# The first keys' sums stay in PSUM banks, B's projection moves behind the first stage, and a fourth shift block is summed along rows

## The chip, the cores and the metric

The kernel runs on one core of a Trainium2 chip. The metric is the device time of the whole program in microseconds. The engines are TensorE (PE, with its weight loads PEld), VectorE (DVE), ScalarE (ACT), GpSimd (POOL) and SyncE (SP), which here only issues DMAs; PSUM has 8 banks of 128 x 512 fp32.

## The reference

Two layers over 256 latent tokens and 256 context tokens of width 2048, all in fp32. The part of the first layer that the change is in:

```python
shift, scale, gate = adaln(c, ada_w[i], ada_b[i])            # silu(c) @ w + b, three parts
h = modulate(rms_norm(x, norm_g[i]), shift[:, None], scale[:, None])
shift_c, scale_c, gate_c = adaln(c_ctx, ada_w[i], ada_b[i])
hc = modulate(rms_norm(ctx, norm_g[i]), shift_c, scale_c)
p = h @ w_in                                                 # 2048 x 14400: Q, gate, z, K, V, x, B, C, dt
pc = hc @ w_in[:, base:]                                     # the context needs K, V, x, B, C, dt only
q = rms_norm(heads(cols(p, COL_Q, ...)), q_norm_g)           # 16 heads of 128
k = rms_norm(heads(cols(p, COL_K, ...)), k_norm_g)
```

Then come neighbourhood attention with the context's keys, a bidirectional SSD scan in 8 groups (its B and C go through a convolution of 5 taps), gating and the output projection. The second layer is a gated short convolution. Only the first layer's start is touched.

## The kernel before

Every fp32 operand is split into a high part (fp32r) and the rest, and a product takes three matmuls: high x high, low x high, high x low. A weight of 512 KB (two row blocks of 128 x 512) is loaded into a raw buffer; ScalarE casts its high part into a place (`split`, line 422) and VectorE subtracts to get the low part (`low_part`, line 429). There are three places (w_95, w_96, w_97 in the listings below). The raw buffers are five, raw_90 to raw_94, and in the first stage four spare ones (two halves of PT, xtm, yi). SP issues all loads in one order; a load waits there until its buffer is free, and the loads behind it wait too.

A planner writes the program: Python tasks ask for an engine and for operands, a model of times (`Plan`) tells when they will be ready, and each instruction is put at the end of its engine's list when the model holds it to be due. What is put there is fixed; each engine runs its list in order.

The first stage starts before the modulated input h is known, and builds it block by block. There are eight blocks of 256 input channels; I count blocks from 1 and the stage's steps j from 0, so block 3 belongs to step 2. For a block, its scale and shift (256 values each, for latent and context) are needed. TensorE makes one of them as a product with the padded conditioning vectors: four loads of 512 KB from ada0, 32 narrow matmuls (`cpad`, line 742), a copy, two transposes and a sum (`ada_gen`). For the blocks in `DOTS` the shift is made by VectorE instead (`dot_gen`): the weights lie transposed, the conditioning vectors are broadcast to all partitions (the two loads `full`, line 850), and eight multiply-and-sum instructions along rows (line 859) and a reduction give the shift. `dot_gen` begins when step 2 begins. Then h of the block is written as hH and hL (lines 780 to 792), and step j adds the block's share to

- K and V of the first four heads, for four tiles of 128 rows (two latent, two context): each tile is six matmuls into a bank, and `part_gen` adds the bank to a running sum in SBUF: ScalarE copies at step 0, VectorE adds later (line 818). K's sums lie in the tiles sz and gt, V's in Vt.
- Q for the two latent tiles, kept in two banks (psQ) over all steps,
- B of the first SSD group (`b_part`), kept in two banks (psB0): twelve matmuls.

So four banks remain for K, V and modulation. A row tile of h needs the token rows transposed first (x, lines 640 to 650); the context's last tile comes late in step 0. After step 7 the stage is over, and the program goes on with the first gate (128 x 256 tiles), the dt columns, C, x and z of the first SSD group, attention heads and so on, each projection with the weights of the whole 2048 rows in a row.

## Time and profile before

| | us |
|---|---|
| runs: median, lowest, highest of 3 | 1741.1, 1739.43, 1741.53 |
| profiled execution: span from first to last instruction | 1738.3 |
| TensorE busy | 1717.7 (99%) |
| VectorE busy | 1253.3 (72%) |
| ScalarE busy | 776.2 (45%) |
| mean granted TensorE clock | 1.000 |

The profiled execution's own time is its span; the median of the runs lies 2.8 us above it. Busy is the time in which at least one instruction of the engine was under way. Matmuls overlap, so two that start 0.23 us apart each show some 0.39 us. In the views of the order of time a line has its start and length, the engine, the line of the kernel, the operation, out<-in, the shape and the count, and in brackets the idle time before it and what ended it. A window's line has, after its length, the busy time and count of PE, PEld, DVE, ACT and POOL, then the granted clock, the busy share of the DMA engines and GB/s.

### The profile page before, as it was taken

How to read it: one execution, taken by the hardware profiler on the slowest of the kernel's cores; microseconds unless marked ns; L12 is line 12 of the kernel's file. 1: busy time of each engine (PE TensorE's matmuls, PEld its weight loads, DVE VectorE, ACT ScalarE, POOL GpSimd, SP SyncE). 2: the span in 40 equal slices, each digit the busy share in tenths (PEclk: the TensorE clock that was granted, in tenths of full speed). 3: DMA queues.
4: the chain of work that ended last, by engine and by line, in shares of the span. 5: the costliest groups of instructions: out<-in, count | busy, mean ns of one | idle time of the engine just before them, and what ended most of it. 6: DMA issues, size and time to landing. Idle time of an engine off the chain costs nothing.

```text
span 1738.3 us, 24820 instructions
## 1 busy us (share of the span) xinstructions
PE 1717.7 (99%) x9255; PEld 1451.5 (84%) x9255; DVE 1253.3 (72%) x2108; ACT 776.2 (45%) x1367; POOL 33.2 (2%) x28
## 2 busy tenths in 40 slices
PE   6999999999999999999999999999999999999999
PEld 4777989889888889888888898888888888888887
DVE  5698787877576877676877687887668667665654
ACT  6434544445243445243435243665445344444442
POOL 0000100001000001000000000000000000000000
PEclk9999999999999999999999999999999999999999
DMA  9987644566754765755766567767867888776763
GB/s 375 366 319 271 206 135 142 180 209 187 228 183 151 234 210 183 227 188 164 230 221 195 191 196 248 258 225 254 280 204 260 267 272 284 246 241 191 248 213 114
DMA packets 192391, 391.03 MB, mean 225 GB/s; under 512 B 16200, under 2 KB 45960, under 8 KB 192016
## 3 DMA queue, kind: packets, MB, share of 16 engines
q1 hardware_dynamic: 184960, 382.88, 67.8%
q10 hardware_dynamic: 7312, 6.59, 1.2%
q8 instruction: 72, 1.18, 0.3%
q14 instruction: 47, 0.39, 0.1%
HBM read 379.79 MB, written 9.62 MB: 224 GB/s over the span
## 4 chain that ended last, share of the span: by engine, by line
PE 96%; DMA 2%; DVE 2%; issue 0%; SPq 0%; ACT 0%; POOL 0%; DVEq 0%; ACTq 0%
PE bank L196 93%; PE bank L200 3%; DMA raw<-in_ada 1%; DMA full<-dram_crow 1%; DVE csb L859 0%; DVE w L429 0%; DVE raw L859 0%; SPq L603 0%; DVE gt L818 0%; DVE yi L859 0%; DVE tmp L623 0%; DVE hL L792 0%; DVE sz L818 0%; DVE tmp L2116 0%; SPq L383 0%
## 5 line engine op out<-in xcount | busy, mean ns | idle before, releaser
L422 ACT CAST w<-raw 128x1024 fp32r<-128x1024 f32 (+1 forms) x344 | 359.8, 1047 | 554.7 <-PE bank L196 462.0
L429 DVE TENSOR_TENSOR w<-raw,w 128x1024 fp32r<-128x1024 f32 (+1 forms) x344 | 417.2, 1216 | 239.5 <-ACT w L422 238.2
L196 PE MATMUL bank<-hH,w 128*128 128x256 f32 (+1 forms) x2064 | 487.0, 325 | 0.0
L196 PE MATMUL bank<-w,hH 128*128 128x512 f32 x1280 | 405.7, 396 | 4.0 <-ACT hH L780 2.5
L196 PEld LDWEIGHTS bank<-hH,w 128*128 128x128 f32 x2064 | 345.3, 188 | 32.1 <-issue 1.7
L196 PE MATMUL bank<-hL,w 128*128 128x256 f32 (+1 forms) x1040 | 335.0, 322 | 0.0
L196 PEld LDWEIGHTS bank<-w,hH 128*128 128x128 f32 x1280 | 237.1, 188 | 56.3 <-DVE gt L818 3.4
L196 PE MATMUL bank<-w,hL 128*128 128x512 f32 x640 | 250.0, 391 | 0.2
L196 PEld LDWEIGHTS bank<-hL,w 128*128 128x128 f32 x1040 | 196.5, 189 | 14.5
L196 PE MATMUL bank<-w,h 128*128 128x512 f32 x768 | 178.2, 390 | 0.0
L196 PEld LDWEIGHTS bank<-w,h 128*128 128x128 f32 x768 | 144.1, 188 | 29.7
L888 DVE CUSTOM_DVE_ANT_0 raw<-raw,csb 128x1024 f32<-128x1024 f32 x128 | 155.3, 1218 | 11.9 <-DMA raw<-in_adaT 9.1
L196 PEld LDWEIGHTS bank<-w,hL 128*128 128x128 f32 x640 | 120.2, 188 | 25.7 <-DVE hL L792 0.9
L196 PE MATMUL bank<-w,mix 128*128 128x512 f32 x588 | 137.8, 391 | 0.0
L196 PEld LDWEIGHTS bank<-w,mix 128*128 128x128 f32 x588 | 109.7, 188 | 22.2 <-issue 0.3
L1371 DVE SCALAR_TENSOR_TENSOR tmp<-bank,cwh,tmp 128x508 f32<-128x508 f32 (+1 forms) x96 | 71.3, 746 | 1.9
L196 PE MATMUL bank<-KL,h 128*128 128x512 f32 x264 | 63.9, 390 | 0.0
L196 PEld LDWEIGHTS bank<-KL,h 128*128 128x128 f32 x264 | 49.5, 188 | 10.2
L196 PE MATMUL bank<-wH,h 128*128 128x512 f32 x168 | 55.7, 391 | 0.0
L196 PE MATMUL bank<-QT,h 128*128 128x512 f32 x168 | 55.7, 391 | 0.0
L429 DVE TENSOR_TENSOR wL<-raw,wH 128x1024 fp32r<-128x1024 f32 x31 | 37.9, 1223 | 23.9 <-ACT wH L422 23.8
L429 DVE TENSOR_TENSOR QL<-raw,QT 128x1024 fp32r<-128x1024 f32 x32 | 39.1, 1223 | 22.1 <-ACT QT L422 21.8
(306 smaller groups left out, 1962.3 us busy)
## 6 DMA issues: line engine op xcount, KB each, us to landing
raw<-in_w_in SPq DMA_DIRECT2D x196, 512.0 KB, 3.8
raw<-in_adaT SPq DMA_DIRECT2D x128, 512.0 KB, 4.8
raw<-in_sc_in SPq DMA_DIRECT2D x128, 512.0 KB, 4.7
raw<-in_w_out SPq DMA_DIRECT2D x64, 512.0 KB, 4.5
raw<-in_ada SPq DMA_DIRECT2D x35, 512.0 KB, 7.7
raw<-in_sc_out SPq DMA_DIRECT2D x32, 512.0 KB, 4.7
raw<-in_w SPq DMA_DIRECT2D x16, 512.0 KB, 5.5
tmp<-dram_csr SPq DMA_DIRECT2D x32, 256.0 KB, 5.2
```

Of the source, the lines that this page charges most:

```text
L196: E(T.matmul(o, l, r, start=start, stop=stop, skip_group_check=True))
L200: E(T.transpose(o, i, ident if k == 128 else ident[:k, :k]))
L422: E(S.copy(H, v))
L429: E(V.tensor_tensor(out=Lo, in0=v, in1=H.bitcast(F32), op=ALU.subtract))
L888: E(V.tensor_tensor_reduce(out=raw, in0=raw, in1=csb, scale=1.0, scalar=0.0, op0=ALU.mult, op1=ALU.add, accum_out=gp[:, h, m:m + 1]))
L1371: E(V.scalar_tensor_tensor(out=do, in0=di, scalar=cwh[:, 32 * k + ch:32 * k + ch + 1], in1=do, op0=ALU.mult, op1=ALU.add))
```

## The change

K's four sums stay in four banks (psK) from step 0 to step 7, as Q's do, and the norm of the keys reads the banks; V is summed as before. That frees sz and gt, which serve as a fourth weight place (wH_101, wL_104) until 24 weights are used, the end of the first stage. K and V tiles alternate in a step. B of the first SSD group is no longer part of the stage: it is projected after the dt columns like the later groups' B, from four loads of 512 KB in place of eight of 256 KB. `DOTS` is 2, 4, 6, 7 in place of 4, 5, 7 (blocks 3, 5, 7, 8 in place of 5, 6, 8), with the weights of these blocks laid out accordingly.

```diff
--- before.py
+++ after.py
@@ -172,10 +172,12 @@
 
 
     xrow = [st([128, D], "KT", name="x0")]
-    QT, Vt, gt = st([128, 4, 256], "QT", F32R), st([128, 4, 512], "Vt"), st([128, 4, 256], "gt")
+    QT, Vt = st([128, 4, 256], "QT", F32R), st([128, 4, 512], "Vt")
+    WH.append(st([128, 1024], "gt", F32R, name="wH3"))
     xrow.append(st([128, D], "KL", name="x1"))
     QL = st([128, 4, 256], "QL", F32R)
-    sz, xtm, yi = st([128, 4, 256], "sz"), st([128, 2, 512], "xtm"), st([128, 4, 256], "yi")
+    WL.append(st([128, 1024], "sz", F32R, name="wL3"))
+    xtm, yi = st([128, 2, 512], "xtm"), st([128, 4, 256], "yi")
     PTs = st([128, 2, 4, 256], "PT")
     PT = [PTs[:, k] for k in range(2)]
 
@@ -360,7 +362,7 @@
     onload = {}
 
     later = deque()
-    DOTS = (4, 5, 7)
+    DOTS = (2, 4, 6, 7)
     started = [False]
     ngem = [0]
 
@@ -394,11 +396,17 @@
 
     lows = deque()
 
-    free_w, in_use = deque(range(NW)), deque()
+    free_w, in_use = deque(range(NW + 1)), deque()
+    NFIRSTW = 24
+
+    def free_place():
+        return next((w for w in free_w if w != NW or pos["split"] < NFIRSTW), None)
 
     def place():
-        in_use.append(free_w.popleft())
-        return in_use[-1]
+        w = free_place()
+        free_w.remove(w)
+        in_use.append(w)
+        return w
 
     def split():
         k = pos["split"]
@@ -457,7 +465,7 @@
         if hold[0]:
             return
         lows_try()
-        while free_w and pos["split"] in RAW:
+        while free_place() is not None and pos["split"] in RAW:
             if plan.ready([RAW[pos["split"]][1]]) > max(plan.t["PE"], plan.t["ACT"]) + 300:
                 return
             split()
@@ -481,6 +489,8 @@
         w = in_use.popleft()
         if w is not None:
             free_w.append(w)
+        if pos["use"] == NFIRSTW:
+            free_w.remove(NW)
         splits_try()
 
 
@@ -537,7 +547,6 @@
     loads.append(lambda: x_load(3))
     loads.append(lambda: E(DMA.dma_start(sm[:, NFIRST:], small[:, NFIRST:])))
     loads.append(lambda: E(DMA.dma_start(cs_[:, CFIRST:], const[:, CFIRST:])))
-    weight(w_in, 0, 2, COL_B, 256)
     q_ada(1)
     dots = deque()
 
@@ -559,7 +568,6 @@
             q_ada(j + 1, *((0,) if j + 1 in DOTS else (0, 1)))
         dot_load()
         w_seg(j, CQ)
-        weight(w_in, j * 256, 2, COL_B, 256)
     loads.append(later_loads)
 
     order = list(range(0, 6)) + list(range(8, 16)) + [6, 7]
@@ -568,7 +576,7 @@
     q_proj(w_in, CG(0), 512)
     for r0 in (0, 1024):
         weight(w_in, r0, 8, COL_DT, 64)
-    for j_ in ssd_cols(0)[1:]:
+    for j_ in ssd_cols(0):
         q_proj(*j_)
     for a in range(1, 4):
         qk = [(w_in, CQ(a), 512), (w_in, CK(a), 512)]
@@ -805,8 +813,6 @@
     statk, statq = st([128, 16], "statk"), st([128, 8], "statq")
 
 
-    szf, gtf = sz.rearrange("p a b -> p (a b)"), gt.rearrange("p a b -> p (a b)")
-    parK = [szf[:, 0:512], szf[:, 512:1024], gtf[:, 0:512], gtf[:, 512:1024]]
     parV = [Vt[:, t, :] for t in range(4)]
 
     def part_gen(j, key, t, o, p):
@@ -920,18 +926,17 @@
             mm(ps, hH[kb][:, tt], HLo[1][:, k], False, last and k == 1)
             pump()
 
-    pars = {"K": parK, "V": parV}
-
-    def kv(j, key, t, HLo):
+    psK = []
+
+    def v_rows(j, t, HLo):
         ps, = banks(1)
-        rows_(j, key, t, ps, HLo, True, True)
-        spawn(urgent, part_gen(j, key, t, pars[key][t], ps))
-
-    def b_part(j):
-        H, Lo = use()
-        for k in range(2):
-            mm_ws(psB0, hH[2 * j + k], hL[2 * j + k], H[:, k], Lo[:, k], 512, j == 0 and k == 0, j == 7 and k == 1)
-        used()
+        rows_(j, "V", t, ps, HLo, True, True)
+        spawn(urgent, part_gen(j, "V", t, parV[t], ps))
+
+    def k_rows(j, t, HLo):
+        if j == 0:
+            psK.extend(banks(1))
+        rows_(j, "K", t, psK[t], HLo, j == 0, j == 7)
 
     for j in range(8):
         need[0] = j
@@ -942,17 +947,15 @@
 
             w3 = [use(k) for k in range(3)]
             psQ = banks(2)
-            psk = banks(2)
+            psK += banks(2)
             for k in range(2):
 
                 for i, (a_, w_) in enumerate(((hH, 0), (hL, 0), (hH, 1))):
                     for t in range(2):
-                        mm(psk[t], a_[k][:, t * 128:(t + 1) * 128], w3[0][w_][:, k], k == 0 and i == 0, k == 1 and i == 2)
-            for t in range(2):
-                spawn(urgent, part_gen(j, "K", t, parK[t], psk[t]))
+                        mm(psK[t], a_[k][:, t * 128:(t + 1) * 128], w3[0][w_][:, k], k == 0 and i == 0, False)
             pump()
             for t in range(2):
-                kv(j, "V", t, w3[1])
+                v_rows(j, t, w3[1])
             for t in range(2):
                 rows_(j, "Q", t, psQ[t], w3[2], True, False)
             for t in range(2, 4):
@@ -962,25 +965,27 @@
                     free_w.append(in_use[2])
                     in_use[2] = None
                     splits_try()
-                for key, k in (("K", 0), ("V", 1)):
-                    kv(j, key, t, w3[k])
+                k_rows(j, t, w3[0])
+                v_rows(j, t, w3[1])
             for k in range(3):
                 used()
-            psB0 = banks(2)
-            b_part(j)
         else:
-            for key in "KVQ":
-                HLo = use()
-                for t in range(2 if key == "Q" else 4):
-                    if key == "Q":
-                        rows_(j, key, t, psQ[t], HLo, False, j == 7)
-                    else:
-                        kv(j, key, t, HLo)
-                used()
-            b_part(j)
-    force(lambda: all(("part", 7, key, t) in got for key in "KV" for t in range(4)), (urgent,))
+            HK = use()
+            for t in range(4):
+                k_rows(j, t, HK)
+                if t == 0:
+                    HV = use(1)
+                v_rows(j, t, HV)
+            used()
+            used()
+            HQ = use()
+            for t in range(2):
+                rows_(j, "Q", t, psQ[t], HQ, False, j == 7)
+            used()
+    force(lambda: all(("part", 7, "V", t) in got for t in range(4)), (urgent,))
     plan.RATE = Plan.RATE
     KT, KL = st([128, 4, 512], "KT", F32R), st([128, 4, 512], "KL", F32R)
+    gt, sz = st([128, 4, 256], "gt"), st([128, 4, 256], "sz")
 
 
     cwh = st([128, 160], "cwh")
@@ -1615,19 +1620,18 @@
 
     Btm[0] = st([128, 2, 4, 128], "Btm", name="Btmt")
     spawn(urgent, first_v())
-    spawn(urgent, kq_gen("K", 0, parK, 4, statk, KT, KL, False), 4)
+    spawn(urgent, kq_gen("K", 0, psK, 4, statk, KT, KL, True), 4)
     spawn(urgent, kq_gen("Q", 0, psQ, 2, statq, QT, QL, True), 2)
 
     def do_g(a, nxt, leave=False):
         psG = banks(2)
         proj(512, 256, psG, nxt, leave)
-        spawn(urgent, silu2_gen("G", a, psG, gt, lambda: attn[0] >= 8 * a and (a or ("K", 0) in got)), 1)
+        spawn(urgent, silu2_gen("G", a, psG, gt, lambda: attn[0] >= 8 * a), 1)
 
     def do_ssd(s, nxt):
-        if s:
-            psB = banks(2)
-            proj(256, 512, psB, 1)
-            spawn(urgent, make_b(s, psB), 3)
+        psB = banks(2)
+        proj(256, 512, psB, 1)
+        spawn(urgent, make_b(s, psB), 3)
         psC, = banks(1)
         proj(256, 256, [psC], 4)
         spawn(urgent, make_c(s, psC), 0, 2)
@@ -1637,11 +1641,10 @@
             spawn(urgent, make_x(s, gi, psX[2 * gi:2 * gi + 2]), 3)
         psZ = banks(2)
         proj(512, 256, psZ, nxt)
-        spawn(urgent, silu2_gen("Z", s, psZ, sz, lambda: ssd_done[0] >= 2 * s and ("K", 0) in got), 1)
+        spawn(urgent, silu2_gen("Z", s, psZ, sz, lambda: ssd_done[0] >= 2 * s), 1)
         for gi in range(2):
             spawn(side, group_gen(s, gi), 4, 4, 3000)
 
-    spawn(urgent, make_b(0, psB0), 3)
     do_g(0, 1)
     for h in range(4):
         spawn(side, head_gen(0, h))
@@ -2194,7 +2197,7 @@
     w0 = np.stack([f('na_ssd_w_in')[0][j * 256:j * 256 + 256, c:c + 512].reshape(2, 128, 512).transpose(1, 0, 2)
                    for j in range(8) for c in (COL_K, COL_V, COL_Q)]).reshape(24, 128, 1024)
 
-    for j in (4, 5, 7):
+    for j in (2, 4, 6, 7):
         for q in range(4):
             k0, c0 = (q % 2) * 1024, j * 256 + (q // 2) * 128
             ada0[8 * j + 4 + q] = f('ada_w')[0][k0:k0 + 1024, c0:c0 + 128].T
```

The planner moves instructions. The first place is ScalarE near the end of step 0: xm is the transposed token rows, bank_85 the last context tile's, hH_297 and hH_304 block 1's h, half_76 the copy of block 2's scale; raw_91 in the changed list is step 1's key weight. DMAHW is the landing of a load. Before:

```order
L816 COPY Vt<-bank_89 128x512 [waits PE_49]
L648 COPY xm_137<-bank_85 128x128 [waits PE_49]
L648 COPY xm_139<-bank_83 128x256 [waits PE_49]
L780 ACTIVATE hH_297<-xm_137,S_155,A_154 128x128 [waits Activation_49]
L780 ACTIVATE hH_304<-xm_138,S_155,A_154 128x128 [waits DVE_49]
L747 COPY half_76<-bank_82 128x256 [waits PE_49]
```

And now:

```order
L822 COPY Vt<-bank_82 128x512 [waits PE_49]
L430 CAST wH_101<-raw_91 128x1024 [waits DMAHW0_49]
L656 COPY xm_137<-bank_85 128x128 [waits PE_49]
L656 COPY xm_139<-bank_84 128x256 [waits PE_49]
L656 COPY xm_141<-bank_82 128x256 [waits PE_49]
L788 ACTIVATE hH_297<-xm_137,S_155,A_154 128x128 [waits Activation_49]
L788 ACTIVATE hH_304<-xm_138,S_155,A_154 128x128 [waits DVE_49]
L755 COPY half_76<-bank_84 128x256 [waits DVE_49,PE_49]
```

The cast of the fourth place's first weight stands ahead of the last context tile's copies.

The second place is SP's list in steps 1 and 2 (in_w is K, V or Q's weight, in_ada modulation, in_w_in B's). Before:

```order
L385 DMA raw_90<-in_w_in 128x2x256
L383 DMA raw_91<-in_w 128x1024
L383 DMA raw_92<-in_w 128x1024
L383 DMA yi<-in_ada 128x1024
L383 DMA raw_93<-in_ada 128x1024
L383 DMA raw_94<-in_ada 128x1024
L383 DMA PT<-in_ada 128x1024
L383 DMA xtm<-in_ada 128x1024
L850 DMA full_773<-dram_crow 128x2048
L850 DMA full_775<-dram_crow 128x2048
```

And now, where PT<-in_w is step 2's value weight and the second PT<-in_ada a piece of block 4's shift that takes its buffer:

```order
L385 DMA raw_91<-in_w 128x1024
L385 DMA raw_94<-in_w 128x1024
L385 DMA PT<-in_w 128x1024
L385 DMA xtm<-in_ada 128x1024
L385 DMA yi<-in_ada 128x1024
L385 DMA raw_91<-in_ada 128x1024
L385 DMA raw_94<-in_ada 128x1024
L385 DMA PT<-in_ada 128x1024
L856 DMA full_639<-dram_crow 128x2048
L856 DMA full_641<-dram_crow 128x2048
```

The vectors' loads stood 58 rows into SP's list and now stand 43 rows into it, two weights and five pieces of modulation behind step 1's query weight (raw_91<-in_w).

The third place is VectorE between step 1's V sums and step 2 (hL_662 is the low part of block 3's h, raw_92 the first piece of block 3's shift weights). Now:

```order
L824 TENSOR_TENSOR Vt<-Vt,bank_84 128x512 [waits PE_49]
L437 TENSOR_TENSOR wL_104<-PT,wH_101 128x1024 [waits DMAHW4_49,PE_49,Activation_49]
L824 TENSOR_TENSOR Vt<-Vt,bank_82 128x512 [waits PE_49]
L865 ISA csb,statk<-raw_92,full_639 128x1024 [waits DMAHW2_49]
L865 ISA raw_92,statk<-raw_92,full_641 128x1024 [waits DMAHW3_49,DVE_49]
...
L865 ISA raw_90,statk<-raw_90,full_641 128x1024 [waits DVE_49]
L874 TENSOR_REDUCE S_155<-statk 128x4 [waits DVE_49]
L875 TENSOR_TENSOR S_155<-S_155,small 128x4 [waits DVE_49]
L800 TENSOR_TENSOR hL_662<-tmp_71,hH_657 128x512 [waits Activation_49]
L800 TENSOR_TENSOR hL_670<-tmp_72,hH_664 128x512 [waits Activation_49]
```

All eight sums for block 3 stand ahead of hL of block 3; before, block 3's shift came from TensorE and the first sums of this kind were block 5's.

## The prediction

> **What bounds the kernel now.** I read the page first (span, busy shares, chain), then the windows of the first 200 us, and then the order of time on TensorE, ScalarE, VectorE and SP inside them.
>
> ```profile
> span 1738.3 us, 24820 instructions
> PE 96%; DMA 2%; DVE 2%; issue 0%; SPq 0%; ACT 0%; POOL 0%; DVEq 0%; ACTq 0%
> 1387.32 88.43 PE bank L196 x390
> 10.00:20.00 10.00, 8.92 (x86) 5.91 (x90) 5.70 (x17) 5.74 (x15) 0.55 (x1) 1.00 1.03 413
> 20.00:30.00 10.00, 8.39 (x51) 5.59 (x40) 7.12 (x17) 7.28 (x14) 0.46 (x1) 1.00 1.04 402
> 30.00:40.00 10.00, 8.25 (x62) 5.40 (x61) 6.74 (x20) 7.69 (x18) 1.52 (x4) 1.00 1.04 399
> ```
>
> The chain that ends last is TensorE for 96% of the span. A stretch of it without a wait has 390 matmuls of 512 columns in 88.43 us, 0.227 us each; I use that price everywhere (six matmuls, one tile of a projection, are 1.36 us). Up to about 45 us the DMA queue sets the pace instead: it is full (1.03 to 1.04 of its engines) at some 400 GB/s, so 512 KB land every 1.3 us. From there on TensorE hardly ever stops. So the span can only change by TensorE work that goes or comes, and by time in which TensorE stands still. I therefore lay out TensorE's time up to the end of the first stage, before and after.
>
> ```profile
> 10.47 2.28 PE L196 MATMUL bank<-raw,cpad 128*32 128x256 f32 x16 [10.47 <-DMA raw<-in_ada]
> 37.25 0.88 PE L200 MATMUL bank<-const,x 128*128 128x128 f32 x6 [0.30 <-ACT x L633]
> 47.80 0.39 PE L196 MATMUL bank<-hH,w 128*128 128x512 f32 x1
> 52.73 0.50 PE L196 MATMUL bank<-w,hH 128*128 128x512 f32 x1
> 57.29 1.93 PE L196 MATMUL bank<-raw,cpad 128*32 128x256 f32 x32
> 59.16 0.50 PE L196 MATMUL bank<-w,hH 128*128 128x512 f32 x1
> 76.45 0.48 PE L196 MATMUL bank<-w,hH 128*128 128x512 f32 x1
> 190.33 0.28 PE L196 MATMUL bank<-hL,w 128*128 128x256 f32 x1
> ```
>
> Here hH,w is B and w,hH is K, V or Q. Step 0's B runs from 47.80, step 1's keys begin at 52.73, step 2's at 76.45, and the first gate's matmul is at about 190.2: that is where the first stage ends, B included. From 57.29 to 59.16 one half of a block's modulation passes: with its two transposes and the change of shape I take 2.1 us for one.
>
> **The work that is left, part by part.** For step 2 onward, from the end of its first key tile (76.45 + 1.4 = 77.9):
>
> ```profile
> L196 PE MATMUL bank<-w,hH 128*128 128x512 f32 x237 | 76.9, 397 | 1.5 <-DVE gt L818 1.5
> L196 PE MATMUL bank<-w,hL 128*128 128x512 f32 x118 | 46.2, 392 | 0.1
> L196 PE MATMUL bank<-hH,w 128*128 128x512 f32 x48 | 16.0, 392 | 0.0
> L196 PE MATMUL bank<-hL,w 128*128 128x512 f32 x24 | 9.4, 390 | 0.0
> L200 PE MATMUL bank<-const,half 128*128 128x128 f32 x10 | 2.0, 278 | 0.4 <-ACT half L747 0.4
> ```
>
> 355 matmuls of K, V and Q are 80.5 us, 72 of B 16.3 us, and the ten transposes stand for five halves of modulation, 10.5 us: 107.3 us. The stretch lasts 190.2 - 77.9 = 112.3 us, so 5.0 us of it are waits, mostly for VectorE's sums. In the changed kernel the same point has the same 80.5 us ahead, all of B (16 x 6 = 96 matmuls, 21.8 us) and six halves (scale and shift of block 6, scale of blocks 5, 7, 8 and the shift of block 4, which the new order puts behind this point), 12.6 us: 114.9 us. The shift of block 3 is the one piece that TensorE never does again, 2.1 us for good.
>
> Now when does TensorE get to that point? Two waits are new.
>
> **First wait: a cast ahead of the rows.** Both kernels are alike up to 37.25. The fourth weight place is empty from the start, so the planner casts step 1's key weight at once: on ScalarE this cast now stands directly ahead of the copies of the last context tile, and its low part on VectorE ahead of that tile's lows. Before, no place was free and the copies went first:
>
> ```profile
> 38.18 0.54 ACT L648 COPY xm<-bank 128x128 f32<-128x128 f32 x2
> 38.60 0.89 ACT L780 ACTIVATE hH<-xm,S,A 128x128 fp32r<-128x128 f32 x2
> 48.68 2.00 ACT L422 CAST w<-raw 128x1024 fp32r<-128x1024 f32 x2
> 39.54 0.29 DVE L792 TENSOR_TENSOR hL<-tmp,hH 128x128 fp32r<-128x128 f32 x1
> 49.76 2.36 DVE L429 TENSOR_TENSOR w<-raw,w 128x1024 fp32r<-128x1024 f32 x2
> 38.12 1.86 PE bank L196 x32
> 41.23 1.86 PE bank L196 x32
> ```
>
> That weight is the ninth load after the context. The eighth before, the last piece of block 2's shift, is multiplied in the stretch 41.23 to 43.09, so it is there at about 42; without B's 256 KB (-0.65 us) and with one more load of 1.3 us the weight lands at 42.4 (estimate, 41 to 44). ScalarE, otherwise free at 38.2, waits for it, casts (1.0) and only then copies and makes the tile's high part: 44.8 in place of 39; VectorE's low part (1.2) lies before hL: 46.9 in place of 39.8. Queued behind on TensorE are that tile's keys, both halves of block 2's modulation, now at 47.5 and 50.9 in place of 38.1 and 41.2, and with them step 1's hH. SP holds more: the next value weight goes into the same buffer as the key weight, so it and all loads behind it issue only when VectorE is done with the key weight, at 46.3. Block 2's shift is complete at 52.8, its chain of copy, transposes, sum, weight and hH takes 3.2 us, and step 1's first keys start at 56.0. Their lows and two pairs of transposes make them end at 59.7. Then come 2.2 us for block 3's scale and seven tiles (9.5 us less the last, V): the fourth key tile of step 1 ends at 70.2. With no first wait it would end at 76.45 less V, Q (4.1), two B (5.4) and three halves (6.3), which is 60.7; that is the lower bound, and 72 the upper one, for a load that lands 2 us later.
>
> **Second wait: the vectors for block 3.** VectorE's sums need the broadcast conditioning vectors (full). They still start with step 2, and block 3 is step 2's own. On SP their two loads stand behind a piece of block 4's shift that takes the buffer of step 2's value weight. That weight's cast goes into the fourth place, which step 1's keys hold until their last tile. So from the end of that tile:
>
> ```profile
> PT<-in_w SPq DMA_DIRECT2D x5, 512.0 KB, 3.5
> full<-dram_crow SPq DMA_DIRECT2D x2, 1024.0 KB, 13.8
> 76.46 1.15 SPq L850 DMA_DIRECT2D full<-dram_crow x2
> 88.43 1.23 DVE L859 CUSTOM_DVE_ANT_0 csb<-yi,full 128x1024 f32<-128x1024 f32 x1 [1.46 <-DMA full<-dram_crow]
> 94.75 1.22 DVE L859 CUSTOM_DVE_ANT_0 raw<-raw,full 128x1024 f32<-128x1024 f32 x1
> 95.89 1.22 DVE L859 CUSTOM_DVE_ANT_0 csb<-raw,full 128x1024 f32<-128x1024 f32 x1
> 106.41 0.15 DVE L868 TENSOR_REDUCE S<-statk 128x4 f32<-128x8 f32 x1
> 60.85 0.60 ACT L780 ACTIVATE hH<-xm,S,A 128x256 fp32r<-128x256 f32 x1 [0.24 <-DVE S L761]
> 66.57 0.69 DVE L792 TENSOR_TENSOR hL<-tmp,hH 128x512 fp32r<-128x512 f32 x1
> ```
>
> cast 1.1, low part 1.2, issue 0.1, the piece 3.5 from issue to landing as the weights of an idle queue (its issues and the two of the vectors, 1.15 together, go on meanwhile), then 2 MB at 400 GB/s 5.2; after that seven sums at 1.15 apart (the first of the eight runs between the two landings) 8.1, sum and bias 0.4: 19.6 us. The shift is there at 89.8. From there hH, its four activations per row block of 0.5 us and the two lows make the first key tile end 5.5 us later, at 95.3 (before, the shift's hH began at 60.85 and the second low ended 6.4 us after that, hidden behind other tiles). In those 25.1 us TensorE has one V tile, Q and block 4's scale to do, 6.2 us, and the tile itself, 1.4; it stands still for 17.5. Bounds: the nearest rows are 13.8 us from issue to landing for the vectors on a busy queue (25 us in all) and, with everything landing 3 us sooner, 16.5.
>
> At the clock: the windows grant 1.00 throughout, also in 10:20, after TensorE had not run for its first 10.47 us, so I add nothing for a restart. [...]
>
> **What gets cheaper.** VectorE sums 28 key tiles less but does eight sums along rows more:
>
> ```profile
> L818 DVE TENSOR_TENSOR gt<-gt,bank 128x512 f32<-128x512 f32 x14 | 9.5, 682 | 0.7 <-PE bank L196 0.7
> L818 DVE TENSOR_TENSOR sz<-sz,bank 128x512 f32<-128x512 f32 x14 | 9.2, 683 | 2.1 <-PE bank L196 2.0
> 90.00:100.00 10.00, 10.00 (x70) 7.37 (x69) 9.90 (x18) 2.52 (x4) 0.00 (x0) 1.00 0.76 256
> ```
>
> 18.7 us go and 8 x 1.15 = 9.2 come, so it is freer in the first stage. V has two banks less, but a K tile lies between two V tiles, so a bank has 4.1 us until it is needed again, 2.5 with a modulation between. Of the 5.0 us of waits after step 2 I leave 1.5 (bounds 0, and 8 where blocks 7 and 8, 18.4 us of sums in a row, hold up V's sums or hL). B behind the first stage runs in the form of the later groups; its 2 MB of loads are hidden behind the gate's matmuls. With that cover gone they would cost 5.2 us.
>
> **The sum.** 95.3 + 114.9 + 1.5 = 211.7 for the end of all this work, against 190.2: +21.5. Everything later is the same work on a TensorE that is never idle for long, so the span goes from 1738.3 to 1759.8. The median shown, 1741.1, lies 2.8 above the profiled span; 1759.8 + 2.8 gives 1762.6, and I say 1762.
>
> **Rivals.** *Both waits are covered; the change does its work.* TensorE loses 2.1 us of work and 3.5 of waits: 1741.1 - 5.6 = 1735.5, faster. It holds if the key weight's cast finds its data landed and block 3's shift is ready 7.6 us after step 1's last key tile; the steps add up to 25.1 there, and vectors loaded before the weights would be needed to get under it. Against it stands the order on SP. Chance 0.05. *Only the first wait is covered* (the load lands before 38): the point moves from 70.2 to 60.7, hence 1762.6 - 9.5 = 1753; for it, the landing time is an estimate; against it, the queue was full until then. Chance 0.14. *Only the second is covered:* 1762.6 - 17.5 = 1745; what would do it, an earlier load of the vectors, is not in the order. Chance 0.05. *VectorE becomes the bound in steps 5 to 7,* or the vectors take the 13.8 us of a busy queue: 6 us more, 1769. For it, VectorE was busy 9.9 of 10 us from 90 to 100; against it, those sums are spread over the steps before. Chance 0.13. *TensorE restarts slowly:* were ten matmuls after each wait at twice their time, 4.5 us more: 1767. [...] Chance 0.05. The forecast keeps 0.58.
>
> **How the numbers follow.** What a measurement here can tell from no change is about 0.2%, 3.5 us. The lower bounds together (60.7, 16.5, no later wait) give 60.7 + 16.5 + 5.5 + 114.9 = 197.6, +7.4: 1748; the upper ones (72, 25, 8) 225.4, +35: 1776. I take 1748 to 1776; beyond it lie the covered waits, 0.1, and a little above. Faster 0.05, same 0.04 (half of "only the second is covered" and some rest), slower 0.91.
>
> **What would show it.** In the changed profile ScalarE should be idle between 38 and 42, its wait ended by the landing of a weight; step 1's first keys should begin near 56; VectorE's first sum along rows should come near 79 and the chain pass through the vectors' load and these sums; TensorE should show one gap of 10 us or more around 77 to 90 and its clock stay 1.00; the gate's first matmul should come near 190, and B behind the dt columns. If step 2's keys begin before 78 in the changed profile, the second wait is wrong, and with it the sign may be.

## The result and the profile after

The changed kernel takes 1772.6 us (median of 4 runs, 1771.84 to 1774.28) against 1740.3 for the kernel before on the same chip: ratio 1.0187, 95% interval 1.0175 to 1.0199. It is 32 us slower. The profiled execution's span is 1771.1 us, 1.5 below the median. Its own time is 1772.9 us: in every run on record the time lies 1.7 to 2.1 us above the span. From its page, then the groups of TensorE's first 200 us, then windows:

```profile
span 1771.1 us, 24683 instructions
PE 1724.3 (97%) x9221; PEld 1453.6 (82%) x9221; DVE 1247.0 (70%) x2092; ACT 772.8 (44%) x1358; POOL 33.4 (2%) x28
PE 94%; DMA 2%; DVE 2%; ACT 1%; issue 0%; SPq 0%; DVEq 0%; ACTq 0%
L198 PE MATMUL bank<-w,hH 128*128 128x512 f32 x240 | 83.4, 410 | 21.8 <-ACT hH L788 20.7 <-DVE xm L657 0.9
...
24.56:27.97 3.41, 3.41 (x9) 2.67 (x10) 3.31 (x5) 3.00 (x6) 0.00 (x0) 0.50 1.02 403
41.70:51.80 10.10, 6.38 (x40) 3.03 (x40) 3.26 (x8) 2.90 (x7) 0.00 (x0) 0.50 0.38 117
83.00:99.00 16.00, 3.89 (x8) 2.28 (x9) 11.33 (x20) 6.19 (x11) 0.00 (x0) 0.50 0.62 225
434.30:437.50 3.20, 3.20 (x17) 3.20 (x16) 3.17 (x6) 0.00 (x0) 2.90 (x1) 0.50 0.48 168
```

TensorE is not busy for 1771.1 - 1724.3 = 46.8 us; before it was 1738.3 - 1717.7 = 20.6. That is 26.2 of the 32.8 us by which the span grew. TensorE's busy time grew by the other 6.6 although 2.1 us of work are gone, so matmuls take 8.7 us longer. The four windows cover nearly all of what ran at a granted clock of 0.50: TensorE is busy there for 16.9 us, and at a granted clock of 1.00 half of that, 8.4, would have done (an estimate: matmuls of 128 x 256 begin 0.213 us apart near 435, at 0.50, and 0.113 apart near 438, at 1.00). Before, no window of the first 200 us had a clock below 1.00. The first of the four delays step 0 by 1.3 us (15.5 us from its first keys to the last rows' transposes at 38.8, 14.2 before), but the weight that lands at 42.1 comes later still.

The order of time on ScalarE, VectorE, SP and TensorE in the changed kernel shows where the waits are (start, length, ..., idle time before and what ended it):

```profile
42.10 1.04 ACT L430 CAST wH<-raw 128x1024 fp32r<-128x1024 f32 x1 [2.23 <-DMA raw<-in_w]
44.31 0.80 PE L198 MATMUL bank<-w,hH 128*128 128x512 f32 x1 [3.72 <-ACT hH L788]
46.22 0.80 PE L198 MATMUL bank<-w,hL 128*128 128x512 f32 x1 [1.11 <-DVE hL L800]
47.37 2.79 PE L198 MATMUL bank<-raw,cpad 128*32 128x256 f32 x24
50.94 1.09 PE L202 MATMUL bank<-const,x 128*128 128x128 f32 x4
58.67 0.50 PE L198 MATMUL bank<-wH,hH 128*128 128x512 f32 x1
72.71 1.05 ACT L430 CAST wH<-PT 128x1024 fp32r<-128x1024 f32 x1 [5.20 <-PE bank L198]
73.80 1.23 DVE L437 TENSOR_TENSOR wL<-PT,wH 128x1024 fp32r<-128x1024 f32 x1 [1.53 <-ACT wH L430]
75.44 0.90 SPq L856 DMA_DIRECT2D full<-dram_crow  x2
81.30 1.23 DVE L865 CUSTOM_DVE_ANT_0 csb<-raw,full 128x1024 f32<-128x1024 f32 x1 [5.68 <-DMA full<-dram_crow]
83.84 1.22 DVE L865 CUSTOM_DVE_ANT_0 raw<-raw,full 128x1024 f32<-128x1024 f32 x1 [1.31 <-DMA full<-dram_crow]
92.54 0.16 DVE L875 TENSOR_TENSOR S<-S,small 128x4 f32<-128x4 f32 x1
93.39 0.80 PE L198 MATMUL bank<-w,hH 128*128 128x512 f32 x1 [14.55 <-ACT hH L788]
95.59 0.80 PE L198 MATMUL bank<-w,hL 128*128 128x512 f32 x1 [1.41 <-DVE hL L800]
433.94 0.63 PE L198 MATMUL bank<-hH,w 128*128 128x256 f32 x2 [1.82 <-DVE w L437]
```

Both waits stand where the prediction put them: the cast at 42.1 that waits for a weight ahead of the last context tile, and the chain from the fourth place (free at 72.7) over the vectors' load to block 3's shift at 92.7, while TensorE stands still for 14.6 us. A third wait, at 433.9, is new.

For the comparisons that follow I divide each profile at the first stage's end (the gate's first matmul, with B's 21.8 us added where B comes later). Before: 190.2 and 1548.1 us behind it. After: 197.9 + 21.8 = 219.7, and 1551.4. So the first stage lost 29.5 us and the rest 3.3.

### The profile page after: what moved, and what is told of

Read it like the earlier page. It is cut to its first block, busy times and chain, and to the rows that moved or that the text cites. A ratio compares the mean times of both kernels' runs of the same rounds, so it can differ in the third digit from the quotient of the medians.

```text
span 1771.1 us, 24683 instructions
## 1 busy us (share of the span) xinstructions
PE 1724.3 (97%) x9221; PEld 1453.6 (82%) x9221; DVE 1247.0 (70%) x2092; ACT 772.8 (44%) x1358; POOL 33.4 (2%) x28
## 4 chain that ended last, share of the span: by engine, by line
PE 94%; DMA 2%; DVE 2%; ACT 1%; issue 0%; SPq 0%; DVEq 0%; ACTq 0%
PE bank L198 91%; PE bank L202 3%; DMA raw<-in_w 1%; DMA raw<-in_ada 0%; DVE w L437 0%; DMA full<-dram_crow 0%; DMA bias<-in_rpb 0%; DMA tmp<-dram_csr 0%; ACT hH L788 0%; DVE csb L865 0%; DVE raw L865 0%; DVE wL L437 0%; ACT w L430 0%; ACT tmp L791 0%; DVE hL L800 0%
## 5 line engine op out<-in xcount | busy, mean ns | idle before, releaser
L437 DVE TENSOR_TENSOR w<-raw,w 128x1024 fp32r<-128x1024 f32 x337 | 410.9, 1222 | 268.8 <-ACT w L430 265.4
L430 ACT CAST w<-raw 128x1024 fp32r<-128x1024 f32 x337 | 354.6, 1053 | 551.1 <-PE bank L198 463.1
L198 PE MATMUL bank<-w,hH 128*128 128x512 f32 x1200 | 384.3, 398 | 21.8 <-ACT hH L788 20.7
L198 PEld LDWEIGHTS bank<-w,hH 128*128 128x128 f32 x1200 | 223.8, 189 | 69.3 <-ACT hH L788 22.0
L198 PE MATMUL bank<-w,hL 128*128 128x512 f32 x600 | 235.5, 393 | 2.9 <-DVE hL L800 2.8
L198 PEld LDWEIGHTS bank<-hL,w 128*128 128x128 f32 x1040 | 197.0, 189 | 14.6
L198 PEld LDWEIGHTS bank<-w,hL 128*128 128x128 f32 x600 | 113.2, 189 | 28.8 <-DVE hL L800 5.1
L198 PEld LDWEIGHTS bank<-KL,h 128*128 128x128 f32 x264 | 49.5, 188 | 10.2
L437 DVE TENSOR_TENSOR wL<-raw,wH 128x1024 fp32r<-128x1024 f32 x34 | 41.5, 1222 | 22.4 <-ACT wH L430 22.3
L430 ACT CAST wH<-raw 128x1024 fp32r<-128x1024 f32 x35 | 36.8, 1052 | 44.4 <-PE bank L198 34.7
```

What stands on the lines that cost most here:

```text
L198: E(T.matmul(o, l, r, start=start, stop=stop, skip_group_check=True))
L430: E(S.copy(H, v))
L437: E(V.tensor_tensor(out=Lo, in0=v, in1=H.bitcast(F32), op=ALU.subtract))
```

## The experiments

All times are medians, the ratios are against the kernel before on the same chip, each with its 95% interval. Its median lay between 1740.2 and 1740.7.

| kernel | us | ratio | stage's end with B | rest |
|---|---|---|---|---|
| before | 1740.3 | | 190.2 | 1548.1 |
| after | 1772.6 | 1.0187 (1.0175 to 1.0199) | 219.7 | 1551.4 |
| after, shifts 5, 6, 8 | 1754.5 | 1.0081 (1.0064 to 1.0097) | 200.6 | 1551.4 |
| after, fourth place later | 1766.6 | 1.0150 (1.0135 to 1.0165) | 217.0 | 1547.8 |
| after, both of these | 1750.9 | 1.0058 (1.0043 to 1.0073) | 197.0 | 1552.3 |
| before, B moved alone | 1766.4 | 1.0150 (1.0135 to 1.0165) | 214.2 | 1550.5 |
| before, shifts 3, 5, 7, 8 | 1762.3 | 1.0124 (1.0109 to 1.0140) | 212.0 | 1547.3 |
| before, shifts 5, 6, 7, 8 | 1747.5 | 1.0039 (1.0024 to 1.0053) | 198.4 | 1547.3 |
| after, place later, shifts 5 to 8 | 1752.9 | 1.0073 (1.0059 to 1.0086) | 200.7 | 1550.4 |
| before, shifts 6, 8 | 1740.4 | 1.0002 (0.9993 to 1.0011) | 190.0 | 1547.7 |
| before, shifts 4, 6, 8, early | 1744.3 | 1.0022 (1.0013 to 1.0030) | 195.0 | 1547.6 |
| after, vectors a step earlier | 1760.9 | 1.0119 (1.0104 to 1.0134) | 212.3 | 1547.1 |
| after, that and place later | 1755.2 | 1.0086 (1.0069 to 1.0102) | 205.1 | 1547.9 |
| after, 77 idle matmuls | 1779.3 | 1.0223 (1.0208 to 1.0239) | 225.8 | 1551.8 |

One profile's stage end carries the chance of when its first loads land: step 0's first keys began at 23.1 us before and between 23.3 and 25.3 in the others.

### Are the two waits the cause? Each undone, and both

Three shifts, of blocks 5, 6 and 8, so that TensorE makes those of 3 and 7 (and VectorE that of 6):

```diff
-    DOTS = (2, 4, 6, 7)
+    DOTS = (4, 5, 7)
```

> The changed kernel with the shifts of blocks 5, 6 and 8 summed along rows, as before the change; block 3's and block 7's shift are again made by TensorE or VectorE as they were. Theory (two separate waits): the second wait goes, that is TensorE's gap of 14.9 us before 93.39, the waits of 2.0 and 0.7 us behind it and about 1.5 us lost at the granted clock of 0.5 in 82.6 to 99.7; block 3's shift costs TensorE 2.1 us again. 1772.6 - 19.1 + 2.1 = 1755.6, range 1752 to 1760, and the vectors' first sum comes behind step 2's keys. Rival A (the queue is late anyway: after the first wait the raw buffers and the loads of block 3 are as late for TensorE as for VectorE): the gap before step 2 stays over 8 us, time over 1765. Rival B (B's place, the banks or the fewer sums are what cost): time stays within 3 us of 1772.6.

1754.5 us, 18.1 less: the theory's number, and both rivals are out. The 14.6 us gap before step 2 is gone; only a wait of 1.1 us for one of V's sums stands near, at 73.3. The edit takes away the early shift and also leaves three shifts in place of four; the number is tested apart further down.

The fourth place only from step 1's value weight on:

```diff
-        return next((w for w in free_w if w != NW or pos["split"] < NFIRSTW), None)
+        return next((w for w in free_w if w != NW or 3 < pos["split"] < NFIRSTW), None)
```

> The changed kernel, but the fourth weight place is offered only from step 1's value weight on, so the cast of step 1's key weight isn't issued ahead of the last context tile's copies. Theory: the first wait goes (3.9 and 1.7 us of TensorE's idle time before 44.31 and 46.22, the half clock from 41.6 to 51.9, the late shift of block 2); step 1's fourth key tile ends near 61 to 64 in place of 72.7, and the second wait keeps its length of about 20 us from there to block 3's shift, since it is counted from that tile. 1772.6 - 9.5 = 1763, range 1759 to 1765. Rival A (the second wait is set by the DMA queue's own progress, not by the place): block 3's shift is ready at 92 as now, the second gap grows by what the first loses, time 1769 to 1773. Rival B: with no early cast, step 1's key weight is late itself and step 1's keys begin no earlier than 58: 1772.

1766.6 us (runs from 1764.2 to 1769.9), 6.0 less, not 9.5, and above the theory's range. The last context tile's keys now come at 40.6, the granted clock is 1.00 from 40 to 60, and the second gap keeps its length (14.7 us), as the theory had it. Rival A is out, and so is rival B, since step 1's keys begin at 51.5. But new waits of 0.5 to 0.9 us stand between 48 and 57: something else was hidden under the first wait.

Both edits together:

> The changed kernel with both edits: three shifts (blocks 5, 6, 8) along rows, and the fourth place from step 1's value weight on. First keys' sums in banks, B behind the first stage and the fourth place stay. Theory (the waits are separate, their costs add): 1772.6 - 17.0 - 9.5 = 1746; and if the slow granted clock comes only from the two long gaps, it reads 1.00 through the first 100 us and 1 to 3 us more go: 1740 to 1748, about the kernel before. The banks and B then are worth nothing or a little (VectorE's 18.7 us of key sums were mostly off the path: at most the 5.0 us of waits after step 2 before the change: 1737). Rival (B behind the first stage or the banks cost by themselves, for instance by the wait of 1.8 us at 433.9 that the kernel before doesn't have): over 1750.

1750.9 us: outside the theory's range and just over the rival's 1750 (one of the four runs took 1748.7). With both waits gone the kernel is still 10.5 us slower than before. TensorE's order of time shows small waits, for block 2's modulation, where the kernel before has none; two windows show what they do to the clock:

```profile
48.54 0.50 PE L198 MATMUL bank<-w,hH 128*128 128x512 f32 x1 [0.92 <-DVE xm L657]
51.20 0.49 PE L198 MATMUL bank<-w,hH 128*128 128x512 f32 x1 [0.79 <-ACT hH L788]
52.42 0.50 PE L198 MATMUL bank<-w,hL 128*128 128x512 f32 x1 [0.73 <-DVE hL L800]
59.74 0.50 PE L198 MATMUL bank<-wH,hH 128*128 128x512 f32 x1 [0.49 <-DVE xm L657]
...
50.00:53.50 3.50, 1.99 (x13) 0.77 (x15) 2.94 (x9) 2.55 (x5) 0.00 (x0) 1.00 1.03 413
53.60:57.00 3.40, 3.40 (x33) 1.74 (x25) 0.21 (x1) 0.37 (x1) 0.00 (x0) 0.50 1.03 416
```

The two profiles differ by 11.0 us: 6.8 in the first stage (197.0 against 190.2) and 4.2 behind it. Before, step 0's B ran from 47.80 to about 50.5, just where these waits are. One more, 1.1 us at 69.7, is for a V bank, of which the change leaves fewer. The next experiment moves B alone.

### Parts of the change made alone in the kernel before

Only B moved behind the first stage (its loads of the stage and its calls there taken out, and projected like the later groups' B):

```diff
-            psB0 = banks(2)
-            b_part(j)
...
-            b_part(j)
...
-        if s:
-            psB = banks(2)
-            proj(256, 512, psB, 1)
-            spawn(urgent, make_b(s, psB), 3)
+        psB = banks(2)
+        proj(256, 512, psB, 1)
+        spawn(urgent, make_b(s, psB), 3)
```

> The kernel before with one part of the change alone: B's weights and matmuls of the first group behind the first stage, in the form of the later groups. Keys' sums stay with VectorE, three shifts along rows, no fourth place. Theory: what is left when both waits are undone (1750.9 against 1740.6) is B's cover that is gone: its tiles stood on TensorE between step 0 and step 1 (from 47.80 to 50.5) and in every later step, and without them the latency of block 2's modulation and of the sums shows, as in that run's waits of 1.1, 1.0, 1.0, 0.6 and 1.3 us between 48 and 70 and the half clock behind them. 1740.6 + 8 = 1749, range 1746 to 1756 (VectorE here also has 18.7 us of key sums that the shorter steps have to cover). Rival A: B's move is free, the 10 us come from the banks that the keys hold (VectorE's release of a V bank, 1.3 us at 69.7) or from the fourth place: time 1738 to 1743.

1766.4 us: 26 us slower, three times the theory's price of 8, and rival A is out too. Most of it lies elsewhere than I thought. Step 1 waits 2.6 us for the low part of its key weight, but step 2 begins at 76.1, as before at 76.4. Then come waits for VectorE's sums along rows:

```profile
51.97 0.51 PE L196 MATMUL bank<-w,hH 128*128 128x512 f32 x1 [2.59 <-DVE w L429]
109.52 0.51 PE L196 MATMUL bank<-w,hH 128*128 128x512 f32 x1 [1.90 <-ACT hH L778]
111.90 0.80 PE L196 MATMUL bank<-w,hL 128*128 128x512 f32 x1 [1.88 <-DVE hL L790]
134.57 0.54 PE L196 MATMUL bank<-w,hL 128*128 128x512 f32 x1 [1.70 <-DVE hL L790]
176.72 0.80 PE L196 MATMUL bank<-w,hL 128*128 128x512 f32 x1 [1.01 <-DVE hL L790]
...
90.00:100.00 10.00, 10.00 (x46) 8.29 (x45) 10.00 (x16) 2.46 (x3) 0.00 (x0) 1.00 1.03 410
100.00:120.00 20.00, 16.09 (x82) 11.45 (x81) 18.49 (x32) 6.30 (x11) 0.00 (x0) 0.83 0.67 219
...
108.67 0.16 DVE L867 TENSOR_TENSOR S<-S,small 128x4 f32<-128x4 f32 x1
```

Block 5's shift is there at 108.8, two us later than before (106.4 plus its bias). But step 4, which began at 114.3 before, has 2.7 us of B less in each of steps 2 and 3 ahead of it, and TensorE is done with step 3 at 107.6. Before:

```profile
114.28 0.50 PE L196 MATMUL bank<-w,hH 128*128 128x512 f32 x1
```

So B was cover: eight times 2.7 us of TensorE's work under which VectorE made sums. Blocks 5, 6 and 8 are all late now, and each group of waits has half clock with it: 0.83 is granted from 50 to 60 and from 100 to 120, 0.91 from 120 to 160 and from 160 to 200, by which I estimate 3.4 us at 0.50 and then three times some 7. The keys' banks take 18.7 us off VectorE. With them, the place that they free (from step 1 on) and the new order of K and V, B behind the stage leaves the kernel 10.5 us slower in place of 26. Which part of this the banks have is not shown: no run has them with B still in the stage, where four for K, two for Q and two for B would take all eight and leave none for V.

Only the four shifts, of blocks 3, 5, 7 and 8:

```diff
-    DOTS = (4, 5, 7)
+    DOTS = (2, 4, 6, 7)
```

> The kernel before, with one part of the change alone: the shifts of blocks 3, 5, 7 and 8 along rows in place of three. Keys' sums stay with VectorE, B stays in the first stage, no fourth place. Theory: the first wait isn't there (step 1's keys begin near 52.7 as before), the second is: the vectors issue where step 2 starts in program order, and from there the load and seven sums take some 17 us; TensorE has B's and Q's tiles to cover part. Second gap of 10 to 18 us before step 2's keys: 1740.3 + 14 - 2.1 = 1752, range 1748 to 1758. Rival A (the second wait came only because step 1's keys held the fourth place, so that the load of the vectors stood behind a buffer): no gap over 3 us, time 1736 to 1742. Rival B (VectorE with all key sums and the row sums becomes the bound in the first stage): further waits of 5 us and more after step 2, over 1760.

1762.3 us, 22 slower and 4 above the theory's range. Rival A is out: without any fourth place there is a gap of 17.8 us before step 2's keys at 88.94. The vectors issue at 71.0 in step 2's place of the program, and VectorE waits for them:

```profile
70.96 0.90 SPq L850 DMA_DIRECT2D full<-dram_crow  x2
76.83 1.22 DVE L859 CUSTOM_DVE_ANT_0 csb<-PT,full 128x1024 f32<-128x1024 f32 x1 [6.27 <-DMA full<-dram_crow]
88.94 0.80 PE L196 MATMUL bank<-w,hH 128*128 128x512 f32 x1 [17.79 <-ACT hH L780]
91.14 0.80 PE L196 MATMUL bank<-w,hL 128*128 128x512 f32 x1 [1.40 <-DVE hL L792]
92.30 1.94 PE L196 MATMUL bank<-raw,cpad 128*32 128x256 f32 x16
```

The gap is at the upper end of the theory's 10 to 18 us, and its sum took 14. It had not counted the wait for hL (1.4 us) nor the half clock from 75.0 on (0.75, 0.50 and 0.73 granted from 70 to 80, 80 to 90 and 90 to 100, some 20.5 us at 0.50), in which TensorE is busy for 5.1 and by my estimate loses half of that: 16 narrow matmuls take 1.94 us at 92.30, where 32 took 1.93 at 57.29 in the kernel before. The time is rival B's (over 1760), but not its mechanism: TensorE's further waits, behind 92, come to 3.4 us where rival B had 5 and more, and to 2.0 in the kernel before.

### Number or position of the shifts?

Four late ones in the kernel before (blocks 5, 6, 7, 8):

```diff
-    DOTS = (4, 5, 7)
+    DOTS = (4, 5, 6, 7)
```

> The kernel before with four shifts along rows, none of an early block: 5, 6, 7 and 8 in place of 5, 6 and 8. It tells number from position. Theory (position: only the early block 3 makes TensorE wait for the vectors): TensorE saves one half of a modulation, 2.1 us, VectorE gets 9.2 us more, part of which shows as waits for its sums near 145 to 190: 1738 to 1744. Rival (number: four blocks are too much for VectorE in the first stage): over 1748, with waits for VectorE of 5 us and more in all after 130.

1747.5 us, between the two. The waits after 130 come to 5.6 us, the rival's sign, though its time does not come out. A late fourth shift costs 7 us, an early one 22: in this kernel position is two thirds of it, number one third. TensorE waits 1.4 us for hL of block 7 near 157, and 1.6, 1.7 and 0.3 for block 8 between 177 and 181.

The same four with the keys in banks, B behind, the place from step 1 on:

> The changed kernel with the fourth place from step 1's value weight on, and four shifts along rows of which none is early: blocks 5, 6, 7 and 8. Against the same kernel with blocks 5, 6 and 8 (1750.9) it adds one late shift. In the kernel before, that one cost 7.1 us, in waits for hH and hL of blocks 7 and 8 (1.7, 0.7, 1.8, 2.0 and 0.7 us near 156 and 177). Theory: that was VectorE's load, and here the 18.7 us of key sums are gone from it: the shift saves TensorE's 2.1 us, 1749, range 1747 to 1751. Rival: the cost is the sums' start behind their own loads and their eight sums in a row, the steps here are shorter (13 to 16 us) than before (17 to 22), and blocks 7 and 8 come late again: over 1754.

1752.9 us, 2.0 over its neighbour with three (1750.9, with runs from 1748.7 to 1752.8), where the theory had 2.1 below and the rival 3 or more above. The late wait is one only (1.6 and 0.3 us for hL of block 8, at 163 and 165), so the load on VectorE probably had a part. How much stays open: TensorE, ScalarE and VectorE run the same instructions in both profiles up to 60 us, and yet the clock granted from 40 to 50 is 0.83 in this one and 1.00 in the other. The last section comes back to that.

```profile
40.00:50.00 10.00, 8.58 (x87) 5.16 (x88) 4.76 (x12) 4.08 (x8) 0.00 (x0) 1.00 0.69 253
40.00:50.00 10.00, 8.71 (x80) 4.39 (x80) 3.76 (x11) 3.50 (x9) 0.00 (x0) 0.83 0.56 204
```

(The upper line is the kernel with three shifts, the lower the one with four.)

Two shifts in the kernel before (`DOTS = (5, 7)`, blocks 6 and 8), and three spread evenly with the vectors a step earlier (`DOTS = (3, 5, 7)`, and `need[0] >= 1` as below), both in search of a kernel that beats it:

> The kernel before with two shifts along rows, of blocks 6 and 8, in place of three. TensorE gets one half of a modulation more (2.1 us), VectorE 9.2 us less. Theory (the waits for VectorE after step 2, 5.0 us in the kernel before, come from the sums along rows of block 5, with VectorE busy 9.9 of 10 us from 90 to 100): they fall to 1 or 2 us and the time is 1740.4 + 2.1 - 3.5 = 1739, range 1737 to 1741. Rival (those waits come from the keys' and values' sums, which stay): 1740.4 + 2.1 = 1742.5, range 1741.5 to 1744.

> The kernel before with the three shifts spread evenly, of blocks 4, 6 and 8, and the vectors' loads a step earlier, ahead of step 1's query weight. Theory: VectorE's sums then lie 40 us apart, each has two steps of cover, the waits for VectorE of 5.0 us after step 2 shrink and nothing is late, if block 4's shift is there by 95, when step 3 begins: 1736 to 1740. Rival: the vectors' 2 MB in the queue put step 1's and step 2's weights 5.2 us later, and block 4's shift is too early as block 3's was: over 1745.

1740.4 us (no difference that can be measured) and 1744.3. Two shifts cost TensorE 2.1 us of work and give about as much back: between 100 and 200 its idle time falls from 2.0 to 0.6 us. Its time is inside the theory's range. The even spread fails on block 4: its shift is late for step 3 at 93.8 (waits of 0.7, 1.7 and 0.9 us, and a granted clock of 0.84 from 90 to 100). There neither the theory's number nor the rival's came out. No kernel here beats the one before.

### The price of the second wait's chain

The vectors' loads and the sums from step 1 on, in the changed kernel:

```diff
-        yield when(lambda: "crow" in got and all(("xm", t, 7) in got for t in (2, 3)) and need[0] >= 2)
+        yield when(lambda: "crow" in got and all(("xm", t, 7) in got for t in (2, 3)) and need[0] >= 1)
```

> The changed kernel, but the broadcast vectors and the sums along rows may start with step 1 in place of step 2, so SP issues the vectors' two loads ahead of step 1's query weight and step 2's weights. Theory (the second wait's price is the chain fourth place, piece, vectors, seven sums, in this order): the vectors' 7.8 us from 75.90 to 83.71 leave the chain, the gap before step 2's keys shrinks from 14.9 to some 7 us, while the 2 MB in the queue cost step 1 nothing where TensorE is late anyway: 1772.6 - 8 = 1764, range 1758 to 1768. Rival (the queue sets the pace of both steps): step 1's weights come 5.2 us later, step 1's fourth key tile ends 5 us later, and nothing is won: 1769 to 1775.

1760.9 us, 11.7 less, within the theory's range. The loads issue at 61.7, the first sum comes at 69.4 and step 2's keys at 84.8, with a gap of 7.6 us in place of 14.6:

```profile
61.66 0.81 SPq L856 DMA_DIRECT2D full<-dram_crow  x2
69.42 1.23 DVE L865 CUSTOM_DVE_ANT_0 csb<-raw,full 128x1024 f32<-128x1024 f32 x1 [1.28 <-DMA full<-dram_crow]
84.78 0.80 PE L198 MATMUL bank<-w,hH 128*128 128x512 f32 x1 [7.62 <-ACT hH L788]
```

Of the 11.7 us the first stage has 7.4 (212.3 against 219.7); the other 4.3 lie behind it, where the wait at 433.9 doesn't come. With the place from step 1 on besides:

> The changed kernel with its four shifts of blocks 3, 5, 7 and 8 kept and both waits eased where they arise: the fourth place from step 1's value weight on, and the vectors' loads and the sums along rows from step 1 on. Theory (the two are separate): 1772.6 - 6.0 (the place alone) - 11.7 (the vectors alone) = 1755, range 1752 to 1757; what is left over the kernel before is B's cover. Rival: step 1 now begins 7 us earlier, the vectors' loads, the pieces and the sums are counted from the queue and don't come earlier by as much, so the gap before step 2 grows back: over 1758.

1755.2 us, the theory's sum. The prices of the two waits add up, and the gap stays at 7.6 us. All four shifts kept, this is the best that I found for the change's own plan; it is 14.5 us slower than the kernel before.

### Does the half clock cost?

77 matmuls that compute nothing that is used, into a bank that nothing needs:

```diff
+    def spin(n, w):
+        ps, = banks(1)
+        for _ in range(n):
+            T.matmul(ps, w[:, 0, 0:128], w[:, 0], start=True, stop=True, skip_group_check=True)
+        give(free_b, ps)
...
+                if t == 3:
+                    spin(15, w3[0][0])
...
+            if j == 2:
+                spin(62, HK[0])
```

> The changed kernel with 77 matmuls more that compute nothing that is used, of 128 x 512 on a weight that is already there, into a free bank: 15 ahead of the last context tile's keys (3.4 us) and 62 ahead of step 2's keys (14.1 us). All else stays in its order. They run while TensorE stands still, so they cost nothing if its clock has no say. Theory (the half clock behind the waits is real time: the half of block 2's modulation at 47.4 takes 3.6 us in place of 1.9, step 2's first tiles run at half speed up to 99.7): the granted clock reads 1.00 from 50 to 100 and the time falls by 2 to 4 us, to 1768.6 to 1770.6. Rival: the granted clock of 0.5 costs nothing, since waits for VectorE and the queue stand behind it: 1771.5 to 1773.5; if the extra matmuls run over into the work, more.

1779.3 us, 6.7 more. As a price of the half clock this run failed, and by my own doing: the bank that the first 15 took was being emptied by the very copies that TensorE waited for, so they began at 44.05, behind the wait, and ran at half speed themselves (6.43 us for 15, 0.43 each, against the 0.227 of the stretch without a wait). What the trace does show is the clock where TensorE is kept at work:

```profile
44.05 6.43 PE L944 MATMUL bank<-w 128*128 128x512 f32 x15 [4.09 <-DVE xm L657]
51.11 1.50 PE L198 MATMUL bank<-raw,cpad 128*32 128x256 f32 x24
80.38 14.35 PE L944 MATMUL bank<-w 128*128 128x512 f32 x62
80.00:90.00 10.00, 10.00 (x52) 8.00 (x43) 5.69 (x9) 0.00 (x0) 0.00 (x0) 1.00 0.59 233
90.00:100.00 10.00, 7.23 (x27) 4.92 (x26) 6.20 (x13) 5.59 (x11) 0.00 (x0) 0.89 0.82 283
```

With TensorE at work through the second wait, busy for 10.00 of 10 us, the clock is 1.00 from 80 to 90 (0.63 in the changed kernel, where it is busy for 0.00), and the 24 narrow matmuls that took 2.79 us there take 1.50 here, behind the 15, with 1.00 granted from 50 to 60. It is 0.89 from 90 to 100 and from 100 to 120, with a wait of 1.7 us for hL at 97.3. Step 2's keys come at 95.1 in place of 93.4, and more waits for modulation follow between 137 and 160, and one of 3 us at 441. What the half clock is worth on the path that sets the end is not measured.

## Why the prediction was right or wrong

**The sign and the two waits: right, and shown.** Going back to three late shifts gave 18.1 us back (one late shift more or less was worth 2.0 in a like kernel, so most of it is block 3's), undoing the early place 6.0; the vectors' part of the second chain, moved ahead, 11.7.

**First wait.** The cast at 42.1, the tile's keys at 44.3 and 46.2, block 2's scale at 47.4 came within 0.7 us of the text. Then half a modulation took 3.6 us in place of 2.1, step 1's keys began at 58.7 (56.0 expected), and the place came free at 72.7 (70.2; the upper bound was 72). The price of the wait, 9.5 us, was wrong. Without it step 2's keys come 5.5 us earlier (87.9 against 93.4), and the first stage ends 2.7 to 3.6 earlier (219.7 - 217.0, and 200.6 - 197.0); the 6.0 us in the whole time also hold the wait at 433.9, which that kernel's profile hasn't. So the point without the wait isn't 60.7. That figure let block 2's modulation run back to back, where the trace without the wait shows waits of 0.5 to 0.9 us.

**Second wait.** From the place to the shift 20.0 us (19.6 expected): 8.4 from the vectors' issue to the last landing, where the text had 8.7 for the piece and the vectors, and 8.5 for the sums. TensorE is idle for 14.6 and, for hL, 1.4 and 0.3: 16.3 us (17.5 expected); the tile ends near 98.5, that is 3.2 us late, 2.5 of them from the first wait.

**The restart: wrong.** The text added nothing, because the windows grant 1.00 after the first 10.47 idle us. The changed kernel ran 3.4 us from 24.6, 10.2 from 41.6, 17.1 from 82.6 and 3.4 from 434.2 at a granted clock of 0.50. The sign was in the profile before, in the matmuls' spacing and not in the clock column:

```profile
13.00:14.00 1.00, 1.00 (x6) 1.00 (x6) 0.00 (x0) 0.60 (x2) 0.00 (x0) 1.00 1.02 410
15.00:16.00 1.00, 1.00 (x12) 1.00 (x11) 0.98 (x3) 0.87 (x3) 0.00 (x0) 1.00 1.01 406
```

Both are transposes of 128 columns, back to back: 4 started in the first microsecond, 0.214 us apart, and 9 in the second, 0.109 apart (the counts include those still under way), and both lines say 1.00. So TensorE did start at half speed after its first idle stretch, of 10.47 us; the first record of the clock in that trace is at 14.19, and the column reads 1.00 ahead of it. Half of TensorE's busy time in the windows from 41.70 and from 83.00, 3.2 and 1.9 us, is my estimate of what the two waits cost by the clock. One piece of it can be read off: 3.57 us for the half of block 2's modulation from 47.37 to 50.94, against 1.87 us for one from 57.29 in the kernel before.

**The rest of the work, 114.9 + 1.5.** It took 121.2 (98.5 to 219.7), 4.8 more, inside the bounds of 0 to 8: 6.3 us beyond the priced work, not 1.5. Here the text mis-sized a term. It took the whole 5.0 us that its prices left over in the kernel before for waits, and let 3.5 of them go with the keys' sums. Idle time was the smaller part of it, before and after:

```profile
77.90:190.20 112.30, 110.30 (x597) 84.87 (x596) 95.54 (x157) 43.29 (x69) 0.00 (x0) 1.00 0.79 286
98.50:197.90 99.40, 96.62 (x561) 72.81 (x560) 77.77 (x132) 41.83 (x79) 0.00 (x0) 0.99 0.80 289
```

TensorE is idle for 2.0 of the 5.0 us in the upper line and for 2.8 of the 6.3 in the lower, and the rest of the half clock, up to 99.7, is worth some 0.6. So about 3 us, before and after, are time that the prices leave out, and the banks could not take them away. The longest idle times end on modulation's copies (1.65 us at 171.0, 0.43 at 152.6), not on the sums that the text feared.

**B moved at no cost: the step that failed most.** The text asked what hides B's loads, and not what B hides. Alone it costs 26 us in the kernel before; with the rest of the change and neither wait the kernel is 10.5 us slower, most of which I put down to B, though one of the waits there is for a V bank. The forecast survived since it counted the work that TensorE has during each wait, B's absence included; the rivals did not. The text priced both waits covered at 1735.5 (measured with both undone: 1750.9), only the first at 1753 (1766.6), only the second at 1745 (1754.5): each 10 to 15 too low, about that price or a little more.

**What comes later, nothing: wrong by 3.3 us.** The wait at 433.9 and its window at half clock came there. So the miss of 10.0 us, from 1762.6 to 1772.6, is 8.0 in the stage and 3.3 behind it, less 1.3 by which profile and median lie closer than the text took them to be (1.5 against 2.8). Both parts are too low and don't make up for each other; the range held because it was wide enough, with 3.4 us to spare.

**The rivals' times.** 1769, VectorE as the bound or slow vectors, came nearest in time and not in cause: the later waits end on modulation's copies, and the vectors took 8.4 us. VectorE did become the bound where the keys' sums stayed and the steps were shortened, with B moved alone.

## What to carry to other kernels

Before moving work off a stage, ask what waits under it: work that is itself on the bound engine may be the only cover that another engine's results have, and its price when moved is what it covered. A job given to a helper engine needs its inputs' loads, in the queue's order, to fit between the last and the next due time; count the chain from the point where its buffer comes free, and give early blocks to the engine that needs no such load. And read a clock off the spacing of like instructions where a profile begins, before trusting its column (here transposes 0.214 and 0.109 us apart, with 1.00 beside both).
